# A decoder layer on one core: 24 of 26 pairs of projection blocks in seven products, the convolution by channel groups, and one weight sum per pair made by an adding DMA

## The chip, the core and the metric

The kernel runs on one core of a Trainium2 chip. TensorE (PE) multiplies matrices, with its weight loads shown apart (PEld); VectorE (DVE), ScalarE (ACT) and GpSimd (POOL) do element-wise work; SyncE (SP) issues most of the transfers, GpSimd some of them. The metric is the time on the device in microseconds (us), the median of several runs, and lower is better. Next to it stands one profiled execution with its own time; all durations of single instructions come from that one.

## What is computed

One layer: RMSNorm of x, one wide projection, three groups of heads, an output projection, a residual and a last RMSNorm. All in float32, with x of 512 tokens by 2048 features.

```python
h = rmsnorm(x, norm_g[l])
proj = h @ w_in[l]                       # 2048 -> 6664 features
(cv_a, cv_b, cv_gate, fq, fk, fv, f_logit, fox_gate,
 mq, mem_gate) = jnp.split(proj, SPLITS, axis=-1)

u = cv_a * jax.nn.sigmoid(cv_b)
u = causal_depthwise_conv(u, conv_w[l], conv_b[l])          # 31 taps, 512 channels
u = jax.nn.silu(layernorm(u, conv_ln_g[l], conv_ln_b[l]))   # over channels
y_conv = (u @ w_conv_pw[l]) * jax.nn.silu(cv_gate)

logf = jax.nn.log_sigmoid(f_logit + b_f[l])
y_fox = fox_attention(fq, fk, fv, logf) * jax.nn.silu(fox_gate)       # 8 heads, causal
y_mem = memory_attention(mq, mk, mv) * jax.nn.silu(mem_gate)          # 4 heads, 256 memory tokens
x = x + jnp.concatenate([y_conv, y_fox, y_mem], -1) @ w_out[l]
```

Before the split, `mk` and `mv` come from a projection of the normalised memory. At the end stands `rmsnorm(x, final_g)`.

## The kernel before

**Precision.** Every float32 operand is split into a high and a low part in a format that TensorE multiplies at once (`whi`/`wlo` of a weight, `hh`/`hl` of the normalised input, kept transposed as feature by token). A product is three matmuls: high by high, high by low, low by high (`mm3`, L104 to L106). A split costs a cast on ScalarE (L93) and a subtraction on VectorE (L94).

**Blocks.** The projection is 52 blocks of 128 output features, in pairs, and a narrow one for the forget logits (L407, L408). A block in the plain form (`project`) streams 512 tokens through 16 feature tiles: 16 x 3 matmuls of 512 columns. Two blocks are a pair.

**Seven products.** `pair` computes two blocks as a 2 by 2 matrix product (two halves of the 2048 features, two halves of the 512 tokens) with seven products instead of eight, each 8 feature tiles x 3 matmuls of 256 columns (`product`, L729). For it, sums of the four quarters of the input are needed in split form: `s0`, `s1`, `s2` (`first_sums`) and a fourth (`last_sum`) that is written over a quarter of the input, `hl` and `hh`, that no plain block may read after that. Each pair also makes four sums of its weights on VectorE (`less`, L699). A weight half is loaded by SyncE into one of six buffers called `raw`.

**Order.** The first 22 blocks and the forget logits run plain: convolution inputs A and B of four channel groups, memory queries, memory gates, convolution gates, and one fox pair. In that stretch the background list `bg` spreads 120 taps of the depthwise convolution (L328) and the cumulative sum of the forget logits over the projections, 6 to 8 items each; the LayerNorm over channels (`centre`, `normalise`, L489 to L514) runs beside the last memory projection, and `first_sums` and `last_sum` beside the convolution gates and the first fox pair. The other 15 pairs then run in seven products, each with the attention work of the pair before it between its products. The output projection (L978) follows.

Tiles get their buffers from pools, and a tile framework puts in the waits and orders the instructions of each engine by when it expects them to be ready. Each engine works its own list in order: an instruction that waits holds back all that stand behind it on that engine.

Of the kernel before, what the change touches and what calls it, by code (L numbers as in the profile page):

```python
# [10 lines left out]
F32 = mybir.dt.float32  # L11
# [23 lines left out]
PLAIN = 1  # L35
# [12 lines left out]
def hybrid_layer_kernel(  # L48
# [58 lines left out]

    bg = deque()
# [40 lines left out]
    cd = dr.tile([NH, S], F32, name="cd")  # L149

# [10 lines left out]
    mkv = mpool.enter_context(tc.tile_pool(name="mkv", bufs=1, side="right"))  # L161
# [5 lines left out]
    with tc.tile_pool(name="start", bufs=1) as st:  # L167
# [129 lines left out]
    def project(f0, per=0):  # L297
# [5 lines left out]
        background(per)  # L303
        return o

    def silu_of(pool, o, tag, bufs):

        sg = pool.tile([P, S], F32, tag=tag, name=nm(tag), bufs=bufs)
        nc.scalar.activation(sg, o, AF.Silu)
        return sg  # L310

# [3 lines left out]
    with tc.tile_pool(name="conv", bufs=1, reuse_waits="tile") as cp:  # L315
        cs = [tuple(cp.tile([P, S], F32R, name=f"cs{w}{c}") for w in "hl") for c in range(NC)]
        acc = [cp.tile([P, S], F32, tag=f"acc{c}", name=f"acc{c}") for c in range(NC)]

        def taps_of(c, up):
            a = acc[c]  # L320

            def first():
                nc.scalar.activation(  # L323
                    a, up[:, 0:S], AF.Identity, scale=cwt[:, c, 0:1], bias=conv_b_c(c)
                )

            def tap(j):
                return lambda: nc.vector.scalar_tensor_tensor(  # L328
                    a, up[:, j : j + S], cwt[:, c, j : j + 1], a, ALU.mult, ALU.add
                )  # L330

            bg.append(first)
            bg.extend(tap(j) for j in range(1, TAPS))

        def conv_in(c):
            oa = project(C_A + c * P, 6)
            ob = project(C_B + c * P, 6)
            up = cp.tile([P, PAD + S], F32, tag="up", name=nm("up"), bufs=3)
            nc.gpsimd.memset(up[:, 0:PAD], 0.0)
            sg = cp.tile([P, S], F32, tag="sgb", name=nm("sgb"), bufs=2)  # L340
            nc.scalar.activation(sg, ob, AF.Sigmoid)
            nc.vector.tensor_tensor(up[:, PAD:], oa, sg, ALU.mult)
            taps_of(c, up)

        def mem_query(ma, h):
            o = project(M_Q + h * P, 7)
            qh = ma.tile([P, S], F32R, tag="qh", name=nm("qh"), bufs=1)
            ql = ma.tile([P, S], F32R, tag="ql", name=nm("ql"), bufs=1)
            split(qh, ql, o)
            return qh, ql  # L350

        def mem_probs(ma, h, q):
            qh, ql = q
            pr = []
            for i2 in range(2):
                sp = at((P, 2, M))
                for j in range(2):
                    sl = slice((2 * i2 + j) * P, (2 * i2 + j + 1) * P)
                    mm3(sp[:, j, :], (qh[:, sl], ql[:, sl]), (mk[0][:, h, :], mk[1][:, h, :]), True, True)
                ng = ma.tile([P, 2], F32, tag="ng", name=nm("ng"), bufs=4)  # L360
                nc.vector.tensor_reduce(ng, sp, AX.X, ALU.max, negate=True)
                nc.vector.tensor_scalar(ng, ng, SC, None, ALU.mult)
                pp = ma.tile([P, 2, M], F32, tag="pp", name=nm("pp"), bufs=2)
                sm = ma.tile([P, 2], F32, tag="sm", name=nm("sm"), bufs=4)
                for j in range(2):
                    nc.scalar.activation(
                        pp[:, j, :], sp[:, j, :], AF.Exp,
                        bias=ng[:, j : j + 1], scale=SC, accum_out=sm[:, j : j + 1],
                    )
                nc.vector.reciprocal(sm, sm)  # L370
                for j in range(2):
                    nc.scalar.mul(pp[:, j, :], pp[:, j, :], sm[:, j : j + 1])
                pr.append(pp)
            return pr

        def mem_attend(ma, h, pr, gate):
            pts = []
            for mt in range(MT):
                tp = at()
                for i in range(NT):  # L380
                    nc.tensor.transpose(
                        tp[:, i * P : (i + 1) * P], pr[i // 2][:, i % 2, mt * P : (mt + 1) * P], ident
                    )
                th = ma.tile([P, S], F32R, tag="th", name=nm("th"), bufs=2)
                tl = ma.tile([P, S], F32R, tag="tl", name=nm("tl"), bufs=2)
                split(th, tl, tp)
                pts.append((th, tl))
            ov = at()
            for mt in range(MT):
                hs = slice(h * P, (h + 1) * P)  # L390
                mm3(ov, (mv[0][:, mt, hs], mv[1][:, mt, hs]), pts[mt], mt == 0, mt == MT - 1)
            nc.vector.tensor_tensor(gate, ov, gate, ALU.mult)
            nc.gpsimd.dma_start(out=yd[12 + h], in_=gate)

        fgs = {}

        def forget_logits(fg):
            wf = fg.tile([P, KT, NH], F32, name="wf")
# [3 lines left out]
            wfs = fg.tile([P, KT, P], F32R, name="wfs")  # L402
# [6 lines left out]
            f2 = fg.tile([2 * NH, S], F32, name="f2")  # L409
            nc.vector.tensor_copy(f2, fo[: 2 * NH, :])  # L410
            fl = fg.tile([NH, S], F32, name="fl")
            nc.gpsimd.dma_start(out=fl, in_=f2[NH : 2 * NH, :])
            fgs.update(f2=f2, fl=fl)

        def log_sigmoid(fg):
            z, e = fgs["f2"][:NH, :], fgs["fl"]
            nc.vector.tensor_tensor(z, z, e, ALU.add)
            nc.vector.tensor_scalar(z, z, bf_t, None, ALU.add)
            nc.vector.scalar_tensor_tensor(e, z, -1.0, z, ALU.mult, ALU.max)
            nc.scalar.activation(e, e, AF.Exp, scale=-1.0)  # L420
            u = fg.tile([NH, S], F32, name="u")
            nc.vector.tensor_scalar(u, e, 1.0, None, ALU.add)
            lu = fg.tile([NH, S], F32, name="lu")
            nc.scalar.activation(lu, u, AF.Ln)
            nc.vector.scalar_tensor_tensor(e, u, -1.0, e, ALU.add, ALU.subtract)
            nc.vector.reciprocal(u, u)
            nc.vector.tensor_tensor(e, e, u, ALU.mult)
            nc.vector.tensor_tensor(lu, lu, e, ALU.subtract)
            HALF = S // 2
            cs = [fg.tile([NH, HALF + S], F32, name=f"cs{i}") for i in range(2)]  # L430
            for t in cs:
                nc.vector.memset(t[:, :HALF], 0.0)
            nc.vector.scalar_tensor_tensor(cs[0][:, HALF:], z, 0.0, lu, ALU.min, ALU.subtract)
            cur, step = 0, 1

            def double(a, b, step):
                return lambda: nc.vector.tensor_tensor(
                    b[:, HALF:], a[:, HALF:], a[:, HALF - step : HALF - step + S], ALU.add
                )

            adds = []
            while step < S:
                adds.append(double(cs[cur], cs[1 - cur], step))
                cur, step = 1 - cur, 2 * step
            c = cs[cur][:, HALF:]
            adds.append(lambda: nc.gpsimd.dma_start(out=cd, in_=c))
            fgs["c"] = c
            for f in reversed(adds):
                bg.appendleft(f)

        def forget_columns():
            c = fgs["c"]
            pc = at((P, NT * NH))
            for i in range(NT):
                nc.tensor.transpose(
                    pc[:, i * NH : (i + 1) * NH], c[:, i * P : (i + 1) * P], ident[:NH, :NH]
                )
            nc.vector.tensor_scalar(ccol.rearrange("p i h -> p (i h)"), pc, -1.0, None, ALU.mult)
        conv_in(0)
        with tc.tile_pool(name="fg", bufs=1, reuse_waits="tile") as fg:  # L460
            forget_logits(fg)
            conv_in(1)
            log_sigmoid(fg)
            conv_in(2)
            forget_columns()
        conv_in(3)
        with tc.tile_pool(name="matt", bufs=1, reuse_waits="tile") as ma:

            gates = []
# [607 lines left out]
```

## Time and profile before

| | us |
|---|---|
| median of 3 runs (871.82 to 873.68) | 873.48 |
| the profiled execution: its own time | 872.15 |
| its span, first to last instruction | 870.3 |
| TensorE busy | 855.7 |
| VectorE busy | 656.8 |
| ScalarE busy | 463.8 |
| GpSimd busy | 37.9 |

Mean granted TensorE clock: 0.995. Transfers: 107.5 MB, 124 GB/s over the span. The span is 1.85 us below the time of the execution. Busy shares are means over stages with different limits, so the stretches matter more: the plain projections lie before about 350 us, the seven-product pairs from there to about 700 us, the output projection behind.

### The profile page before, as it was taken

What the parts mean: (1) busy time and instruction counts of PE and PEld (TensorE: products, weight loads), DVE (VectorE), ACT (ScalarE), POOL (GpSimd) and SP (SyncE); (2) the same over time, 40 slices, a digit from 0 to 9 for tenths busy, and PEclk for the clock granted to TensorE, in tenths of its full rate; (3) what the DMA queues carried; (4) which work ended last, traced back from release to release, by engine and by line L of the source; (5) the groups of instructions that cost most, each with busy time, mean ns of one, the idle gap of its engine ahead of it and who ended that gap; (6) DMA issues with size and microseconds to landing.
All of it is one profiled execution on the core that took longest, in us unless ns stands there. A gap on an engine that the chain in (4) does not pass through costs nothing.

```text
span 870.3 us, 13950 instructions
## 1 busy us (share of the span) xinstructions
PE 855.7 (98%) x5562; PEld 774.9 (89%) x5562; DVE 656.8 (75%) x948; ACT 463.8 (53%) x734; POOL 37.9 (4%) x76
## 2 busy tenths in 40 slices
PE   8999999999999999999999999999999999999996
PEld 6887887888888888999999999999999988998995
DVE  4656699999956987877777777777777895876964
ACT  5894342225456643577565665657574852443523
POOL 1001000000000002010001000000000000000001
PEclk9999999999999999999999999999999999999998
DMA  9972234333342334243434343333334745351415
GB/s 325 352 193 57 73 97 111 97 78 92 85 109 62 108 97 134 73 121 98 111 88 117 97 103 101 100 95 103 109 98 126 262 154 186 98 194 49 146 49 193
DMA packets 143265, 107.52 MB, mean 124 GB/s; under 512 B 3892, under 2 KB 126816, under 8 KB 142560
## 3 DMA queue, kind: packets, MB, share of 16 engines
q1 hardware_dynamic: 141696, 102.52, 40.4%
q0 software_dynamic: 1504, 4.11, 1.4%
q8 instruction: 43, 0.70, 0.3%
q14 instruction: 22, 0.18, 0.1%
HBM read 98.46 MB, written 8.14 MB: 122 GB/s over the span
## 4 chain that ended last, share of the span: by engine, by line
PE 96%; DVE 1%; issue 1%; DMA 1%; ACT 0%; SPq 0%; POOL 0%; POOLq 0%; ACTq 0%
PE pj L729 34%; PE pj L104 13%; PE pj L105 13%; PE pj L106 13%; PE pj L978 8%; PE at L104 3%; PE at L106 3%; PE at L105 3%; PE at L817 1%; DMA raw<-in_w_mem_kv_dram 1%; PE pj L262 0%; PE at L262 0%; PE pj L407 0%; PE pj L408 0%; PE at L778 0%
## 5 line engine op out<-in xcount | busy, mean ns | idle before, releaser
L93 ACT CAST whi<-raw 128x1024 fp32r<-128x1024 f32 x205 | 214.9, 1050 | 302.6 <-PE pj L105 115.1
L94 DVE TENSOR_TENSOR wlo<-raw,whi 128x1024 fp32r<-128x1024 f32 x205 | 250.2, 1222 | 121.2 <-ACT whi L93 116.7
L105 PE MATMUL pj<-hl,whi 128*128 128x512 f32 x352 | 139.6, 396 | 0.0
L106 PE MATMUL pj<-hh,wlo 128*128 128x512 f32 x352 | 139.4, 396 | 0.0
L104 PE MATMUL pj<-hh,whi 128*128 128x512 f32 x352 | 139.3, 396 | 0.0
L729 PE MATMUL pj<-hh,whi 128*128 128x256 f32 x480 | 135.4, 282 | 0.0
L729 PE MATMUL pj<-hl,whi 128*128 128x256 f32 x480 | 135.0, 281 | 0.0
L729 PE MATMUL pj<-hh,wlo 128*128 128x256 f32 x480 | 134.8, 281 | 0.0
L699 DVE TENSOR_TENSOR raw<-raw,raw 128x1024 f32<-128x1024 f32 x76 | 92.6, 1219 | 0.7
L729 PEld LDWEIGHTS pj<-hh,whi 128*128 128x128 f32 x480 | 90.5, 188 | 0.1
L729 PEld LDWEIGHTS pj<-hl,whi 128*128 128x128 f32 x480 | 90.5, 188 | 0.1
L729 PEld LDWEIGHTS pj<-hh,wlo 128*128 128x128 f32 x480 | 90.5, 188 | 0.0
L328 DVE SCALAR_TENSOR_TENSOR acc<-up,cwt,acc 128x512 f32<-128x512 f32 x120 | 84.5, 744 | 1.2 <-ACT acc L323 0.9
L978 PE MATMUL pj<-whi,rh 128*128 128x256 f32 x448 | 79.9, 279 | 0.7 <-DVE sst L1032 0.4
L104 PEld LDWEIGHTS pj<-hh,whi 128*128 128x128 f32 x352 | 66.1, 188 | 15.9 <-DVE hl L97 0.2
L106 PEld LDWEIGHTS pj<-hh,wlo 128*128 128x128 f32 x352 | 66.1, 188 | 15.7
L105 PEld LDWEIGHTS pj<-hl,whi 128*128 128x128 f32 x352 | 66.2, 188 | 15.5
L978 PEld LDWEIGHTS pj<-whi,rh 128*128 128x128 f32 x448 | 68.8, 188 | 1.3 <-DVE res L904 1.1
L978 PE MATMUL pj<-wlo,rh 128*128 128x256 f32 x224 | 62.3, 279 | 0.0
L978 PEld LDWEIGHTS pj<-wlo,rh 128*128 128x128 f32 x224 | 42.1, 188 | 0.2
L729 PE MATMUL pj<-s0l,whi 128*128 128x256 f32 x120 | 34.4, 286 | 0.0
L729 PE MATMUL pj<-s0h,whi 128*128 128x256 f32 x120 | 34.3, 286 | 0.0
(295 smaller groups left out, 1676.7 us busy)
## 6 DMA issues: line engine op xcount, KB each, us to landing
raw<-in_w_in_dram SPq DMA_DIRECT2D x104, 512.0 KB, 3.8
raw<-in_w_out_dram SPq DMA_DIRECT2D x32, 512.0 KB, 4.6
raw<-in_w_mem_kv_dram SPq DMA_DIRECT2D x12, 512.0 KB, 7.3
xr<-in_x_dram SPq DMA_DIRECT2D x4, 1024.0 KB, 7.9
res<-in_x_dram SPq DMA_DIRECT2D x8, 512.0 KB, 7.2
out_dram<-res SPq DMA_DIRECT2D x16, 256.0 KB, 2.7
rs<-yd SPq DMA_DIRECT2D x15, 256.0 KB, 4.9
mr<-in_mem_dram SPq DMA_DIRECT2D x8, 256.0 KB, 7.3
```

The source lines that it names most:

```text
L93: ins = nc.scalar.copy(hi, src)
L94: nc.vector.tensor_tensor(lo, src, hi.bitcast(F32), ALU.subtract)
L104: nc.tensor.matmul(o, ah, bh, start=start, stop=False)
L105: nc.tensor.matmul(o, ah, bl, start=False, stop=False)
L106: nc.tensor.matmul(o, al, bh, start=False, stop=stop)
L328: return lambda: nc.vector.scalar_tensor_tensor(a, up[:, j : j + S], cwt[:, c, j : j + 1], a, ALU.mult, ALU.add)
L699: nc.vector.tensor_tensor(o, p, q, ALU.subtract)
L729: nc.tensor.matmul(o, p[:, k, :], q, start=start and k == 0 and i == 0, stop=k == HK - 1 and i == 2, skip_group_check=True,)
L817: nc.tensor.transpose(tp[:, (i - j) * P : (i - j + 1) * P], pr[i][:, j * P : (j + 1) * P], ident)
L978: nc.tensor.matmul(o[:, m, :], p, q[:, k, :], start=start and k + m + i == 0, stop=k == HK - 1 and i == 2, skip_group_check=True,)
```

## The change

The plain form is left to five blocks of work: C_A0, C_B0, the forget logits, M_Q0 and M_G0. The remaining 24 pairs all run in seven products, in this order: three memory pairs, then fox pairs of queries with keys (qk) and gates with values (gv), with the pairs C_A, C_B of the other channel groups put between, then the two pairs of convolution gates (g0, g1), and the last qk and gv.

- `first_sums` for all four groups stand ahead of M_Q0 and M_G0, `last_sum` right behind them, and log-sigmoid, cumulative sum and `forget_columns` after that. All sums are thus made at the start.
- The depthwise convolution goes by channel groups: `conv_channels(c, ...)` puts 31 taps of one group on the list, of which each product of a pair takes one (`background(1)`). The accumulated group goes to DRAM (`accd`) and is loaded again (`la`) before the LayerNorm.
- `centre` and `normalise` follow g0, `project_conv` follows g1. Squares for the variance move from VectorE to ScalarE.
- A pair has five loads instead of four. One weight sum, `added`, is made by a GpSimd transfer with `accum_op=ALU.add` onto a loaded buffer, and the rest are three sums on VectorE (`plus`) along a chain.
- The scaling of the rows of x by their norm goes from ScalarE to VectorE.

```diff
-            nc.scalar.mul(xrows[t], xrows[t], rs)
+            nc.vector.tensor_scalar(xrows[t], xrows[t], rs, None, ALU.mult)
...
+    with tc.tile_pool(name="fg", bufs=1, reuse_waits="tile") as fg:
+        oa, ob = project(C_A), project(C_B)
+        conv_channels(0, [oa], ob)
+        forget_logits(fg)
+        with tc.tile_pool(name="stmp", bufs=2, reuse_waits="tile") as stmp:
...
+            for g in range(4):
+                first_sums(tmp, g)
+            oq, og = project(M_Q), project(M_G)
+            for g in range(4):
+                last_sum(tmp, g)
+        forget_columns(log_sigmoid(fg))
...
+        b11, chain, b22, b21, added = (
+            load(f, half) for f, half in ((fa, 0), (fb, 0), (fb, 1), (fa, 1), (fb, 0))
+        )
+        nc.gpsimd.dma_start(out=added, in_=rows(fb, 1), accum_op=ALU.add)
+        x1, zo, x2 = (pj((P, M)) for _ in range(3))
+        product(x1, b11, a11, start=True)
+        yield
+        nc.scalar.copy(x2, x1)
+        plus(chain, b11)
+        product(zo, chain, s1, start=True)
+        p5 = kept(zo, "p5")
+        plus(chain, b22)
+        product(x2, chain, s2)
+        u2 = kept(x2, "u2")
+        product(x1, b21, a12)
+        product(zo, b22, s4)
+        product(x2, added, s3)
+        col = pp_.tile([P, S], F32, tag="col", name=nm("col"), bufs=2)
+        negated_less(col[:, M:], x2, p5)
+        negated_less(col[:, :M], zo, u2)
+        plus(chain, b21)
+        yield
+        product(x2, chain, a22)
+        yield (x1, x2), col
...
+    def open_norm():
+        lp = ln["pool"] = lnpool.enter_context(tc.tile_pool(name="ln", bufs=1, reuse_waits="tile"))
+        background(len(bg))
+        acc = ln["acc"] = [lp.tile([P, S], F32, name=f"la{c}") for c in range(NC)]
+        for c in range(NC):
+            nc.gpsimd.dma_start(out=acc[c], in_=accd[c])
...
+            if i == 0:
+                centre()
+                normalise()
+            else:
+                project_conv()
+                lnpool.close()
+                open_fox()
...
+    work = [(M_Q + h * P, M_G + h * P, after_mem(h)) for h in range(1, NM)]
+    for h in range(NH):
+        work.append((F_Q + h * P, F_K + h * P, after_qk(h)))
+        work.append((F_G + h * P, F_V + h * P, after_gv(h)))
+        if h in (0, 2, 4):
+            c = h // 2 + 1
+            work.append((C_A + c * P, C_B + c * P, after_conv(c)))
+        if h == NH - 2:
+            for i in range(2):
+                g = C_G + 2 * i * P
+                work.append((g, g + P, after_gates(i)))
```

Three places show how the instructions move. The first is on VectorE, behind the forget matmuls. Before, the copy of the forget logits `f` is followed by taps (`acc`), the forget chain, and the splits of the next plain block's weights (`wlo`):

```order
L410 COPY f_1045<-pj_1012 16x512 [waits PE_49]
L328 SCALAR_TENSOR_TENSOR acc_872<-up_998,cwt,acc_872 128x512 [waits DVE_49] x3
L417 TENSOR_TENSOR f_1045<-f_1045,fl 8x512 [waits DMASW7_49]
L328 SCALAR_TENSOR_TENSOR acc_872<-up_998,cwt,acc_872 128x512 [waits DVE_49]
L418 TENSOR_SCALAR f_1045<-f_1045,bf_t 8x512 [waits DMASW5_49,DVE_49]
```

And now, with the temporaries `t` of `first_sums`, whose first rows read the input's parts:

```order
L396 COPY f_1025<-pj_1036 16x512 [waits PE_49]
L315 TENSOR_TENSOR t_119_1075<-hh_105,hl_106 128x512
L315 TENSOR_TENSOR t_120_1076<-hh_113,hl_114 128x512
L315 TENSOR_TENSOR t_121_1077<-hh_105,hl_106 128x512
L315 TENSOR_TENSOR t_122_1090<-hh_107,hl_108 128x512
L315 TENSOR_TENSOR t_123_1091<-hh_115,hl_116 128x512
```

All sums now stand behind the copy, and the copy waits for TensorE. Some sixty rows on, the end of the same list: the last sum's low parts (`hl`), taps, and the steps of the cumulative sum (`cs`) in turn.

```order
L93 TENSOR_TENSOR hl_110<-t_149_1271,hh_109 128x2x256
L371 SCALAR_TENSOR_TENSOR acc_1021<-up_1020,cwt,acc_1021 128x512
L93 TENSOR_TENSOR hl_112<-t_151_1278,hh_111 128x2x256
L421 TENSOR_TENSOR cs_1286<-cs_1287 8x512
L371 SCALAR_TENSOR_TENSOR acc_1021<-up_1020,cwt,acc_1021 128x512
L421 TENSOR_TENSOR cs_1287<-cs_1286 8x512
```

The second place is TensorE at the other end of these: the fifth product of the first pair in seven products, which reads `hl` as it is written, then the transposes of `cs`, then the sixth product.

```order
L500 MATMUL pj_1376<-hl_110,whi_1501 128x256 [waits DVE_49]
L500 MATMUL pj_1376<-hh_109,wlo_1502 128x256
...
L500 MATMUL pj_1376<-hl_112,whi_1501 128x256 [waits DVE_49]
L500 MATMUL pj_1376<-hh_111,wlo_1502 128x256
...
L432 MATMUL at_1311<-ident,cs_1287 128x8 [waits DVE_49]
L432 MATMUL at_1311<-ident,cs_1287 128x8 x3
L500 MATMUL pj_1377<-s2h_884,whi_1530 128x256 [waits Activation_49]
```

In TensorE's list nothing but the two plain blocks M_Q0, M_G0 and the first five products stands between the forget matmuls and these transposes. The third place is TensorE around the variance (`mean_r` multiplies by 1/512). Before, the two matmuls stand among a memory gate's projection (`pj_2383`):

```order
L483 MATMUL pj_2310<-csh_864,mean_r 128x512 [waits DVE_49]
L104 MATMUL pj_2383<-hh_101,whi_2373 128x512
L105 MATMUL pj_2383<-hl_102,whi_2373 128x512
L106 MATMUL pj_2383<-hh_101,wlo_2374 128x512
...
L484 MATMUL pj_2310<-csl_865,mean_r 128x512 [waits DVE_49]
```

Now they are followed at once by the pointwise convolution, which reads the first normalised group (`csh_7594`):

```order
L500 MATMUL pj_7248<-hh_119,wlo_7547 128x256
L615 MATMUL at_7338<-csh_7334,mean_r 128x512 [waits DVE_49]
L616 MATMUL at_7338<-csl_7335,mean_r 128x512 [waits DVE_49]
L103 MATMUL pj_7577<-csh_7594,whi_7583 128x512 [waits Activation_49]
L103 MATMUL at_7578<-csh_7594,whi_7583 128x512 [waits PE_49]
```

No product stands between the variance and that group any more.

More of the change, by code (lines that the diff above doesn't have):

```diff
@@ new lines, in hybrid_layer_kernel, with less, plus @@
+    ppool = ctx.enter_context(ExitStack())
+    pp_ = ppool.enter_context(tc.tile_pool(name="pair", bufs=1, side="right", reuse_waits="tile"))
+    a11 = [quarter(g, 0, 0) for g in range(4)]
+    a12 = [quarter(g, 1, 0) for g in range(4)]
+    a22 = [quarter(g, 1, 1) for g in range(4)]
+    s4 = [quarter(g, 0, 1) for g in range(4)]
+    s1, s2, s3 = sums
+    def less(o, p, q):
+        nc.vector.tensor_tensor(o, p, q, ALU.subtract)
+    def plus(o, p):
+        nc.vector.tensor_tensor(o, o, p, ALU.add)
```

760 lines of the change are left out of this document (356 added, 404 removed).

## The prediction

> **What bounds the kernel now.** I read the busy table first, then the chain of waits, then stretches of the program, then single engines inside those stretches.
>
> ```profile
> PE 855.7 (98%) x5562; PEld 774.9 (89%) x5562; DVE 656.8 (75%) x948; ACT 463.8 (53%) x734; POOL 37.9 (4%) x76
> PE 96%; DVE 1%; issue 1%; DMA 1%; ACT 0%; SPq 0%; POOL 0%; POOLq 0%; ACTq 0%
> ```
>
> TensorE (PE) is busy for 855.7 of 870.3 us and 96% of the chain lies on it, so the kernel is matmul time plus about 15 us of gaps. The next question is whether any other engine is close behind, and where.
>
> ```profile
> 69.00:100.00 31.00, 31.00 (x140) 24.86 (x140) 15.19 (x23) 10.62 (x14) 3.18 (x4) 1.00 0.28 70
> 100.00:150.00 50.00, 50.00 (x218) 40.10 (x217) 47.69 (x65) 16.25 (x17) 1.03 (x2) 1.00 0.33 86
> 150.00:200.00 50.00, 50.00 (x222) 40.54 (x221) 47.47 (x68) 14.54 (x16) 0.12 (x1) 1.00 0.34 89
> 250.00:300.00 50.00, 50.00 (x230) 40.84 (x229) 34.97 (x52) 30.42 (x48) 1.08 (x2) 1.00 0.33 87
> 300.00:350.00 50.00, 50.00 (x217) 40.50 (x216) 41.44 (x60) 19.84 (x30) 5.44 (x8) 1.00 0.38 109
> 400.00:450.00 50.00, 50.00 (x414) 49.65 (x413) 37.98 (x58) 33.11 (x59) 2.17 (x5) 1.00 0.36 96
> ```
>
> Columns: length, then busy time of PE, weight load, VectorE (DVE), ScalarE, GpSimd, then PE clock, DMA share, GB/s. PE is full in every one of them. DVE is not far off: 47.7 and 47.5 of 50 us while the convolution taps run (100 to 200), and 41.4 while the input sums are made (300 to 350). The kernel before has room for its DVE work only because it is spread over hundreds of microseconds of plain projections. The change removes most plain projections, so DVE is what I follow.
>
> **The matmul saving.**
>
> ```profile
> 73.48 0.47 PE pj L104 x2
> 430.65 14.20 PE pj L729 x120
> ```
>
> On the chain, two 512-column matmuls take 0.47 us, 0.2335 each to more places, and 120 of 256 columns take 14.20, 0.1183 each. A plain pair is 96 of the first, 22.4 us; a pair in seven products is 7 x 8 x 3 = 168 of the second, 19.9 us. Nine more pairs take the second form (24 instead of 15): 864 x 0.2335 = 201.7 us go, 1512 x 0.1183 = 178.9 come, a saving of 22.9 us. Every other matmul is as before. If nothing else waited, that would be all.
>
> **The sums at the start.** Before, the four groups of sums of the normalised input were needed at about 340 us. Now the first pair that needs them comes right after five plain blocks' work (C_A0, C_B0, forget logits, M_Q, M_G). In VectorE's new order all sums, the log-sigmoid chain and the taps of channel group 0 stand behind the copy of the forget logits, which waits for the forget matmuls. Call their end t_F.
>
> ```profile
> 100.17 0.39 PE L408 MATMUL pj<-hl,wfs 128*128 128x512 f32 x1
> 100.40 0.40 PE L104 MATMUL pj<-hh,whi 128*128 128x512 f32 x1
> ```
>
> t_F was 100.4 before and should be near that again, since the same blocks stand ahead. From t_F to the first consumer that needs them all (the transposes of forget columns ahead of the sixth product), VectorE has 52 element-wise operations of 128x512 of the sums, 11 of 128x1024 (8 splits of weights, 3 weight sums), 18 taps, and 19 operations of the forget chain, one of them a reciprocal. Prices by their starts in the queue:
>
> ```profile
> 107.10 1.23 DVE L94 TENSOR_TENSOR wlo<-raw,whi 128x1024 fp32r<-128x1024 f32 x1
> 108.24 0.75 DVE L328 SCALAR_TENSOR_TENSOR acc<-up,cwt,acc 128x512 f32<-128x512 f32 x1
> ...
> 109.38 0.73 DVE L328 SCALAR_TENSOR_TENSOR acc<-up,cwt,acc 128x512 f32<-128x512 f32 x1
> 110.04 0.67 DVE L425 SCALAR_TENSOR_TENSOR fl<-u,fl 8x512 f32<-8x512 f32 x1
> 110.65 0.73 DVE L328 SCALAR_TENSOR_TENSOR acc<-up,cwt,acc 128x512 f32<-128x512 f32 x1
> 111.31 3.33 DVE L426 RECIPROCAL u<-u 8x512 f32<-8x512 f32 x1
> 114.57 0.64 DVE L328 SCALAR_TENSOR_TENSOR acc<-up,cwt,acc 128x512 f32<-128x512 f32 x1
> ```
> ```profile
> 303.60 0.68 DVE L556 TENSOR_TENSOR t<-hh,hl 128x512 f32<-128x512 f32 x1
> 304.20 0.69 DVE L94 TENSOR_TENSOR s1l<-t,s1h 128x512 fp32r<-128x512 f32 x1
> 304.93 0.69 DVE L556 TENSOR_TENSOR t<-hh,hl 128x512 f32<-128x512 f32 x1
> 305.65 0.69 DVE L562 TENSOR_TENSOR t<-t,t 128x512 f32<-128x512 f32 x1
> ```
>
> From start to start: a wide one 1.14, a tap 0.66, a small one 0.61, the reciprocal 3.26, an element-wise one of the sums 0.60 or, mostly behind a dependent one, 0.72; I take 0.66. The sums are 52 x 0.66 = 34.3, the wide ones 11 x 1.14 = 12.5, the taps 18 x 0.66 = 11.9, the forget chain 3.3 and 18 small ones, some shorter than 0.61, 10.2: together 72 us. With 0.60 it is 69, with every full duration 78. In the same time PE has M_Q and M_G (22.4), and of the first pair five products of 24 x 0.1183 = 2.84: 36.6 us. So PE, which ran out of nothing here before, waits 72 - 36.6 = **35 us** (32 to 41). The least I can think of: if half of the taps and forget operations were not ahead of the last sums, 13 us fewer, so 22. The stall does not come back: PE stays the bound afterwards and VectorE's early finish buys nothing.
>
> **The LayerNorm over channels.** Before, its chain ran beside memory projections with PE full (250 to 300 above). Now the gate pair g0 is followed by centring and normalising, and g1 by the pointwise convolution, whose first matmul stands directly behind the variance matmuls in PE's order: PE has nothing between.
>
> ```profile
> L505 ACT ACT_TABLE_LOAD x1 | 1.3, 1283 | 0.0
> L506 ACT ACTIVATE up<-up 128x512 f32<-128x512 f32 x1 | 0.6, 635 | 0.0
> L514 ACT ACTIVATE acc<-acc,cols 128x512 f32<-128x512 f32 x4 | 3.2, 824 | 0.0
> L93 ACT CAST csh<-acc 128x512 fp32r<-128x512 f32 x4 | 2.3, 617 | 0.0
> L507 DVE TENSOR_TENSOR up<-up,up 128x512 f32<-128x512 f32 x1 | 0.7, 693 | 0.7 <-ACT up L506 0.7
> L511 DVE TENSOR_TENSOR acc<-acc,up 128x512 f32<-128x512 f32 x4 | 2.5, 686 | 0.0
> ```
>
> Add epsilon 0.4; Ln and Exp, each a table load and 0.63, 3.8; three operations on VectorE 2.1; the product with the first group 0.7; a table load and Silu 2.1; the cast 0.6: 9.7 us, plus about 0.8 of handing over, **10.5 us** (6 if table loads run ahead in the waits, 14 if VectorE is behind).
>
> **The adding DMA.** One weight sum of each pair leaves VectorE; in its place come a fifth load and a GpSimd transfer that adds 512 KB onto it.
>
> ```profile
> raw<-in_w_in_dram SPq DMA_DIRECT2D x104, 512.0 KB, 3.8
> rv<-in_w_mem_kv_dram SPq DMA_DIRECT2D x4, 512.0 KB, 8.1
> wf<-in_w_in_dram POOLq DMA_DIRECT2D x1, 64.0 KB, 3.8
> L699 DVE TENSOR_TENSOR raw<-raw,raw 128x1024 f32<-128x1024 f32 x76 | 92.6, 1219 | 0.7
> ```
>
> The trace has no adding transfer. Bounds: 3.8 us, as a plain load; 8.1, as 512 KB on a crowded queue. The sum is needed by the pair's sixth product, and its buffer comes free with the sixth product of the pair before, some 20 us earlier (a pair's PE time); cast and split (2.3), load (3.8) and issue take up about 7, so about 13 are left. I take nothing; beyond 13, each microsecond is paid in 23 pairs. In the steady pairs VectorE has 3 instead of 4 sums of 1.22, plus 7 taps (4.6): 38.0 of 50 us before becomes 15 to 21 us per pair of 20 to 24 us of PE. It fits, narrowly in three pairs with nine taps, so nothing either (0 to 4 in all). The Trainium skill, page "Collectives: The Full Stack", says of its reduction that the add needs two source reads where a copy needs one; by an estimate from that, twice the 3.8 us, 7.6, would fit as well; no run here shows an adding transfer.
>
> **Small ones.** The row scaling of x moves from ScalarE to VectorE, where PE idled at 62 to 66 us:
>
> ```profile
> 62.00:64.00 2.00, 0.56 (x6) 0.32 (x3) 1.75 (x4) 2.00 (x4) 0.00 (x0) 1.00 0.97 247
> 64.00:66.00 2.00, 1.59 (x11) 1.12 (x11) 2.00 (x5) 2.00 (x4) 0.00 (x0) 1.00 1.00 262
> ```
>
> At most 1.9 us; I take -1. Against it, the clock:
>
> ```profile
> 6.00:8.00 2.00, 0.53 (x5) 0.29 (x3) 0.00 (x0) 0.44 (x1) 0.00 (x0) 1.00 1.03 373
> 8.00:10.00 2.00, 0.96 (x2) 0.58 (x3) 1.36 (x2) 2.00 (x5) 0.00 (x0) 0.63 1.06 400
> 10.00:12.00 2.00, 2.00 (x7) 1.61 (x7) 2.00 (x4) 1.04 (x3) 0.00 (x0) 0.51 1.05 409
> 12.00:14.00 2.00, 2.00 (x10) 1.57 (x10) 1.55 (x3) 1.02 (x2) 0.00 (x0) 1.00 1.05 385
> ```
>
> After PE stood still around 7 us, the granted clock was 0.63 and 0.51 for 4 us: 2 x 0.37 + 2 x 0.49 = 1.7 us of work lost. Two long waits at least, the start and the LayerNorm, make +3 (0 to 6). The same rows show 385 to 409 GB/s; a new pair asks for 6 x 512 KB in 20 us, some 160, so loads have room. The Trainium skill, "TensorE: Matmul & The Clock Gate", Part 1, states a rule that speaks against this change: after an idle window of about 3.4 us PE drops to half clock, and needs about as long busy to return. By that rule each long wait costs an estimated 1.7 us more; the rows at 8 to 12 us agree.
>
> **Sum.** The profiled execution took 872.15 us. 872.15 - 22.9 + 35 + 10.5 - 1 + 3 = 896.8. The median of the runs, 873.48, is 1.3 above the profiled one, the smallest of my errors; I forecast **896 us**, rounded down, with an own range of 880 to 914 from the bounds of the terms.
>
> **Rivals.**
>
> (1) *Faster.* PE waits at neither place and only the saving counts: 872.15 - 22.9 = 849.3, with some waits 850 to 858. For it: PE is 96% of the chain, and the same sums were hidden before. Against: they were hidden under 250 us of plain work, and 69 us of queue do not fit into 37. It decides if the sums' work ahead of the last sum is under about 40 us. Chance 0.14.
>
> (2) *The start costs half.* Splits and sums run ahead of taps and the forget chain, or the LayerNorm finds PE work: 22 + 5 in place of 45.5 give 878, and 868 if each is a little less. Chance 0.13.
>
> (3) *The adding DMA is slow.* With several transfers beside it, it takes 15 to 17 us; sixth products wait 2 to 4 us in 23 pairs, 46 to 92 more: 920 to 985. For it: GpSimd's queue is in order and holds mask operations and stores of outputs ahead of some of these transfers, so one late store delays an add. Against: the DMA share in the steady pairs was 0.36. Slower, chance 0.10.
>
> (4) *The change does not do what it says*, the extra pairs being bound by VectorE (94% of the PE time in three pairs): the 22.9 us are not gained, 872 + 47.5 = 920. Chance 0.05.
>
> The forecast has 0.58.
>
> **How the numbers follow.** Changes under 0.2% (1.7 us) cannot be told from none here. Faster: all of (1) and a quarter of (2), 0.17; same: 0.04; slower: 0.79. The range that leaves 2 in 10 out takes half of (2), the own range and the beginning of (3): 864 to 918.
>
> **What would show it.** Right: PE busy near 833 us and idle of 50 us or more; in the stretch from 100 to 175 us VectorE full and PE half idle, its waits named by the sums' low parts (s0l, s1l, hl) and the cumulative sum; a PE gap of about 10 us right before the pointwise convolution, granted clock under 1 after both; from 200 to 700 us PE full. Wrong: PE full at 100 to 175 us (rival 1); the first weight split of each sixth product ended by a DMA on GpSimd's queue (rival 3); gaps at the chain sums in every pair (rival 4).

## The result, and the profile after

The changed kernel takes 925.51 us (four runs, 921.98 to 927.12) against 873.3 for the kernel before beside it: 1.060 times as long, 95% interval 1.056 to 1.063. It is slower, as forecast, but by 52 us and not by 23: the forecast of 896 and its range of 864 to 918 are both missed.

The first three fences are of the kernel after. The busy table and the beginning of the chain by engine:

```profile
PE 849.9 (92%) x6210; PEld 802.8 (87%) x6210; DVE 705.9 (76%) x1013; ACT 511.2 (55%) x805; POOL 88.3 (10%) x108
PE 62%; DVE 13%; DMA 10%; ACT 7%; issue 7%; POOL 0%; SPq 0%; ACTq 0%; POOLq 0%; DVEq 0%
```

TensorE's share of the chain fell from 96% to 62%. Its idle time in the span of 924.0 us is 74.1 us, where it was 14.6 of 870.3. Busy time fell by 5.8 us and not by 22.9, since matmuls at half clock and the first ones after each wait last longer. Transfers, which had 1% of the chain, have 10%; the forecast had nothing for them.

The windows in which TensorE is not full, with columns as in the prediction:

```profile
125.00:150.00 25.00, 11.48 (x60) 10.07 (x60) 25.00 (x34) 8.83 (x11) 0.00 (x0) 0.70 0.25 63
150.00:175.00 25.00, 11.33 (x74) 11.09 (x75) 24.86 (x40) 7.49 (x11) 2.11 (x2) 0.61 0.33 55
...
650.00:675.00 25.00, 19.45 (x143) 18.86 (x142) 19.73 (x25) 10.86 (x16) 1.60 (x1) 0.86 0.48 111
675.00:700.00 25.00, 10.28 (x50) 8.58 (x49) 12.78 (x17) 12.24 (x16) 0.00 (x0) 0.73 0.26 63
```

At the start VectorE is full, TensorE has less than half of its time and the clock is 0.70 and 0.61. At 650 to 700 us, around the LayerNorm, TensorE is idle for 20.3 us: 14.7 of it are its own two waits (`csh`, `csl` below), and 5.4 belong to a weight split of the pair ahead of it. And what TensorE waited for, in total, times, and longest:

```profile
PE pj L500 <- ACT p L471: 14.7, 1, 14.7
PE pj L103 <- ACT csh L92: 10.1, 1, 10.1
PE pj L500 <- DVE wlo L93: 9.5, 9, 2.0
...
PE pj L500 <- DVE s1l L93: 4.9, 1, 4.9
PE at L616 <- DVE csl L613: 4.6, 1, 4.6
```

The first is the fifth product at the start (the copy that it is put down to stands in ScalarE's list behind the casts of the last sum), the second the pointwise convolution, the third belongs to the steady pairs.

### The profile page after: what moved, and what is told of

Its sections match the earlier page's. It is cut to its first block, busy times and chain, and to the rows that moved or that the text cites. A ratio compares the mean times of both kernels' runs of the same rounds, so it can differ in the third digit from the quotient of the medians.

```text
span 924.0 us, 15570 instructions
## 1 busy us (share of the span) xinstructions
PE 849.9 (92%) x6210; PEld 802.8 (87%) x6210; DVE 705.9 (76%) x1013; ACT 511.2 (55%) x805; POOL 88.3 (10%) x108
## 3 DMA queue, kind: packets, MB, share of 16 engines
q0 software_dynamic: 27104, 18.79, 13.4%
## 4 chain that ended last, share of the span: by engine, by line
PE 62%; DVE 13%; DMA 10%; ACT 7%; issue 7%; POOL 0%; SPq 0%; ACTq 0%; POOLq 0%; DVEq 0%
PE pj L500 31%; PE pj L1013 7%; DMA raw<-in_w_in_dram 7%; PE pj L103 4%; PE pj L104 4%; PE pj L105 4%; DVE wlo L93 4%; PE at L103 3%; PE at L105 3%; PE at L104 3%; ACT whi L92 2%; DVE acc L371 2%; DMA yd<-mgate 1%; DVE raw L467 1%; ACT L803 1%
## 5 line engine op out<-in xcount | busy, mean ns | idle before, releaser
L500 PE MATMUL pj<-hh,whi 128*128 128x256 f32 x768 | 218.5, 285 | 15.5 <-ACT p L471 14.7
L500 PE MATMUL pj<-hh,wlo 128*128 128x256 f32 x768 | 217.3, 283 | 0.0
L500 PE MATMUL pj<-hl,whi 128*128 128x256 f32 x768 | 217.1, 283 | 0.0
L509 POOL DMA_DIRECT2D raw<-in_w_in_dram x24 | 37.7, 1570 | 359.6 <-DMA raw<-in_w_in_dram 104.3
L500 PE MATMUL pj<-s1h,wlo 128*128 128x256 f32 x192 | 58.1, 303 | 9.5 <-DVE wlo L93 9.5
L500 PE MATMUL pj<-s1h,whi 128*128 128x256 f32 x192 | 56.8, 296 | 9.5 <-ACT whi L92 7.3
L500 PE MATMUL pj<-s1l,whi 128*128 128x256 f32 x192 | 56.6, 295 | 4.9 <-DVE s1l L93 4.9
L500 PE MATMUL pj<-s0h,wlo 128*128 128x256 f32 x192 | 54.3, 283 | 0.0
L500 PE MATMUL pj<-s2h,whi 128*128 128x256 f32 x192 | 54.1, 282 | 0.0
L500 PE MATMUL pj<-s2h,wlo 128*128 128x256 f32 x192 | 54.1, 282 | 0.0
```

The source lines that it names most:

```text
L500: nc.tensor.matmul(o, p[:, k, :], q, start=start and k == 0 and i == 0, stop=k == HK - 1 and i == 2, skip_group_check=True,)
L509: nc.gpsimd.dma_start(out=added, in_=rows(fb, 1), accum_op=ALU.add)
```

## The experiments

Three suspects: VectorE's queue at the start, the LayerNorm's chain, and the steady pairs with their adding transfers, which the prediction had priced at nothing. First, one run each, and two for the start.

**Taps left out.**

```diff
-        bg.extend(tap(j) for j in range(1, TAPS))
+        bg.extend(tap(j) for j in range(1, TAPS if c else 1))
```

> The 30 taps of channel group 0 are left out (its convolution is not computed), so VectorE's list between the forget logits and the last sum loses 17 taps of 0.66 us. Theory A (VectorE's queue at the start sets the stall): that stretch goes from 65 us to about 54, the wait ahead of the fifth product shrinks by 11 us, and the kernel takes 912 to 915. Theory B (the wait there is on something else, a transfer, the reciprocal or ScalarE's list): no change, 924 to 926.

Measured: 922.64 us. The fifth product starts at 156.1 us and not at 163.7, and its wait falls from 14.7 to 10.3, so the place is right. The gain of 2.9 us lies within the spread of the change's four runs and in neither theory's range: of the 7.5 us, little or nothing reaches the end. In the trace the first memory head's softmax now makes TensorE wait (1.6), and the steady pairs have 5 us more of idle time between 300 and 650 us than after has (15.2 against 10.0), with the same instructions. So what is gained at the start is in part spent further on; what is near the bound there comes below.

**More cover.**

```diff
-            oq, og = project(M_Q), project(M_G)
-            for g in range(4):
-                last_sum(tmp, g)
...
+    for h in range(3):
+        oq, og = project(M_Q + h * P), project(M_G + h * P)
+        after_mem(h)([oq], og)
+    for g in range(4):
+        last_sum(tmp, g)
...
-    work = [(M_Q + h * P, M_G + h * P, after_mem(h)) for h in range(1, NM)]
+    work = [(M_Q + h * P, M_G + h * P, after_mem(h)) for h in range(3, NM)]
```

> Two more memory pairs run plain (22 pairs in seven products instead of 24), and the last sum comes after them, so TensorE has 45 us more of work that needs no sums. Matmuls cost 2 x 2.54 = 5.1 us more. Theory A (VectorE's queue): the queue to the last sum grows from 67 to about 106 us because it takes in the splits of the added blocks, TensorE's cover from 36 to about 85, so the stall falls from 32 to about 20 and the half clock goes: 925 - 12 - 3 + 5 = 915. Theory B (the wait is on something that does not move with cover): 930.

Measured: 917.54. Eight microseconds better with 5.1 more of matmuls; the stall moves with the cover, as theory A has it. TensorE's longest wait at the start is now 8.5 us for the cumulative sum. Two pairs fewer also mean two adding transfers fewer, about 2 us by the price found below.

**Pointwise convolution one pair later.**

```diff
     def after_qk(h):
-        return lambda xs, col: pr.update({h: probs(h, *queries_keys(xs, col))})
+        def f(xs, col):
+            if h == NH - 1:
+                project_conv()
+                lnpool.close()
+                open_fox()
+            pr.update({h: probs(h, *queries_keys(xs, col))})
+        return f
```

and the same three calls go from the work that follows g1.

> The pointwise convolution moves one pair later, to the beginning of the work that follows qk7, so that a pair's 20 us of products stands between the variance matmuls and it. Theory A (TensorE stands still there only because nothing is left to do): the 14.7 us of idle time between 675 and 700 us and about 3 us of half clock go, 907 to 910. Theory B (the load of the pointwise weights or the loads of the convolution groups are late whatever stands there): at most 5 us come back, 920.

Measured: 917.40. The wait for `csh` falls from 10.1 to 1.5 us and that for `csl` is gone, so the 14.7 us were the missing work behind the variance. Eight of them reach the end, less than theory A's 15 to 18 and more than theory B's 5. Its waits of TensorE show what stayed and grew:

```profile
PE pj L500 <- DVE wlo L93: 11.8, 12, 3.0
PE pj L500 <- ACT whi L92: 7.6, 4, 5.4
```

The 5.4 us is the third product of the pair g1: its weight sum waits for a load that takes 10.8 us in the kernel after, while an adding transfer, a store and four reloads of convolution groups are on the way. That belongs to the next suspect.

**The sum on VectorE in place of the adding transfer.**

```diff
-        nc.gpsimd.dma_start(out=added, in_=rows(fb, 1), accum_op=ALU.add)
...
         plus(chain, b22)
+        plus(added, b22)
```

> The adding transfer becomes a sum on VectorE, as a fourth sum per pair; the fifth load stays. Theory A (the adding transfers delay the plain loads beside them and cost most of the 13 us of waits between 175 and 650 us, and 5 at 650): 910 to 916, though VectorE has 29 us more work. Theory B (VectorE is close to the bound in these pairs, and the transfer does what it is meant to): waits for VectorE grow, 925 to 945.

Measured: 912.07 (909.45 to 914.69), 13 us better although VectorE is busy 23.5 us longer. The edit that was to relieve VectorE costs more than the work that it takes away.

**Neither of the two.** The same without the added line.

> The adding transfer is left out with nothing in its place, so one of the seven products of each pair uses an incomplete weight sum. VectorE keeps three sums per pair, the fifth load stays. If the adding transfer costs time by itself and a fourth sum on VectorE is free: the same as with the sum on VectorE, 908 to 914, idle time of TensorE between 175 and 650 us near 5. If the fourth sum costs too: 898 to 906. If the adding transfer costs nothing and the gain with the sum on VectorE came from elsewhere: 920 to 926.

Measured: 899.04. So the adding transfer costs 26.5 us, where the prediction had nothing, and a fourth sum on VectorE 13.0 (10 to 16 by the spread of the two runs with it). In the steady pairs (280 to 630 us), first the kernel after, then this one:

```profile
280.00:630.00 350.00, 339.30 (x2782) 334.96 (x2782) 289.31 (x409) 224.79 (x350) 46.01 (x50) 1.00 0.66 147
```
```profile
280.00:630.00 350.00, 350.00 (x2910) 348.17 (x2909) 298.02 (x418) 219.87 (x348) 25.69 (x38) 1.00 0.50 136
```

Without the transfer TensorE is never idle and does 128 matmuls more in the same time; the share of the transfer engines falls from 0.66 to 0.50. Which product waits is in the groups of after by form, 300 to 600 us:

```profile
L500 PE MATMUL pj<-s1h,wlo 128*128 128x256 f32 x104 | 31.0, 298 | 7.9 <-DVE wlo L93 7.9
...
L500 PE MATMUL pj<-s2h,whi 128*128 128x256 f32 x104 | 29.2, 281 | 0.0
```

`s2` is the sixth product, the one that uses the added sum: it never waits. `s1` is the third, which uses the second sum along the chain, made by VectorE from plain loads. VectorE's waits for those loads, between 275 and 640 us, in after and in the run without the transfer:

```profile
DVE raw L467 <- DMA raw<-in_w_in_dram: 21.1, 10, 4.5
```
```profile
DVE raw L467 <- DMA raw<-in_w_in_dram: 6.5, 5, 2.1
```

The adding transfer is in time for its own product: no cast and no split waits for it anywhere. It makes other loads late. In the kernel after, 15 sums wait for a load between 175 and 660 us; 14 of these loads are on the way together with an adding transfer and take 5.4 to 10.8 us, while the 46 loads from 280 to 630 us without one beside them take 3.9 (median). Most loads are hardly slower, 4.3 us against 4.2 in the run without the transfer (medians of that stretch); it is the few that a sum waits for that count. VectorE's list is in order, so a sum that waits for a load holds the splits behind it.

**All that only moves the sums.** Two runs tried to take the stall at the start by order alone. In the first, the first sums are written ahead of C_A0; in the second the forget logits also come behind M_G0, and the taps of group 0 last. The lines of the first (its temporaries get a pool at each of the two places):

```diff
+            for g in range(4):
+                first_sums(tmp, g)
         oa, ob = project(C_A), project(C_B)
...
         forget_logits(fg)
...
-            for g in range(4):
-                first_sums(tmp, g)
             oq, og = project(M_Q), project(M_G)
```

> The sums that need no plain block's result (the first three of each group) are written ahead of C_A0 instead of behind the forget logits, so VectorE's list can take them from about 70 us on, beside C_A0, C_B0 and the forget matmuls; matmuls are the same. Behind the copy of the forget logits stand 35 operations, about 25 us, in place of 97. Theory A (the queue behind the copy is the stall): PE's wait at the start falls from 28 us idle and 5 of half clock to under 8: 897 to 903. Theory B (the work is only moved and VectorE is late all the same): 915 to 925.

Measured: 915.46, ten us better than the change and in theory B's range.

> The first sums ahead of C_A0 as in the run with early sums, and the forget logits behind M_G0 in place of ahead of M_Q0, so that the split of their weights no longer holds TensorE while the sums are made; taps of group 0 are written last. Theory A (VectorE's queue, which in the run with early sums only moved its wait of 21 us to the forget matmuls): the wait there goes, some 10 us stay at the fifth product, 900 to 906. Theory B: the wait turns up again at another place, 912 to 918.

Measured: 926.78, no better than the change and outside both ranges. TensorE's waits at the start, first of the one with early sums, then of the other:

```profile
PE pj L395 <- DVE wfs L94: 21.0, 1, 21.0
```
```profile
PE pj L505 <- ACT p L476: 8.6, 1, 8.6
PE pj L394 <- DVE wfs L93: 5.8, 1, 5.8
PE pj L505 <- DVE col L109: 2.7, 1, 2.7
```

`wfs` is the split of the forget weights, now behind the sums in VectorE's list; the room for these weights is also taken over from the temporaries of the sums, which is my edit's doing: with early sums their load is issued at 104.0 us and not at 61.3. So the run is no clean test of the order alone. The wait turns up where the first result of VectorE is needed. In the kernel after, VectorE is busy for 95 us between 60 us and the transposes at 169, and TensorE's matmuls there are worth 74 at full clock (37.5 to t_F, 36.6 behind it). Early sums fill VectorE's free time between 60 and 100 us (busy 38.1 of 40 us, 26.6 before the edit), which goes with the ten us gained; the difference of some 21 us stays as long as all of this work stands ahead of the transposes. Why the second order loses the ten us again was not traced.

**Combinations.** Sum on VectorE with the later convolution, and the two with early sums.

> Sum on VectorE and pointwise convolution one pair later. If the two losses are apart, the gains add: 925 - 13 - 8 = 904. If both are the same crowd of transfers at 640 to 680 us: 909 to 912.

Measured: 907.18, between the two; the later convolution brings 4.9 here, not 8, so the two losses may overlap in part (the two runs with the sum on VectorE are 5 us apart, so this is rough).

> The two and the early sums. If the three losses are apart and the early sums take the stall away: 904 - 25 = 879, near the kernel before; all that is then left of the 22.9 us of matmul time would be eaten by shorter waits. If the losses overlap: 890 to 900.

Measured: 901.64, 5.5 for the early sums and short of both forecasts: the early sums take little of the stall away, as above.

**What is dear in the transfer.** It stays, but writes and does not add:

```diff
-        nc.gpsimd.dma_start(out=added, in_=rows(fb, 1), accum_op=ALU.add)
+        nc.gpsimd.dma_start(out=added, in_=rows(fb, 1))
```

> The GpSimd transfer stays, from the same queue and on the same buffer behind the same load, but it writes and does not add, so one weight sum lacks a part. Theory A (it is the adding that is dear: by the queue's share of the transfer engines an adding 512 KB occupies them for 4.4 us, a plain one 1.8): most of the 26 us go, 902 to 908, landing near 4 us. Theory B (the chain of load, GpSimd's queue and landing holds a buffer too long, whatever the transfer does): little changes, 919 to 926.

Measured: 907.13. Of the 26.5 us the addition as such has 18.4, as theory A has it; another 8.1 is the price of a plain transfer of 512 KB more per pair. Issues and queue of GpSimd's transfers, adding first (packets, MB, share of 16 engines; the last row of each has KB and us to landing):

```profile
q0 software_dynamic: 27104, 18.79, 13.4%
...
raw<-in_w_in_dram POOLq DMA_DIRECT2D x24, 512.0 KB, 7.9
```
```profile
q0 software_dynamic: 5600, 18.79, 6.6%
...
raw<-in_w_in_dram POOLq DMA_DIRECT2D x24, 512.0 KB, 5.0
```

Without the transfer the queue has 2144 packets and 1.9%. So 24 adding transfers make 24,960 packets, 1040 each, and take 13.4% of 924.0 less 1.9% of 896.2, which is 107 us of all 16 engines, 4.4 each. A plain one makes 144 packets and takes 6.6% of 905.7 less the same, 1.8 each. Adding the same bytes occupies the engines 2.5 times as long. The landing (5.0 for 7.9 us) and GpSimd's time for the issue fall with it, so this run does not show how much of the 18.4 us each of the three has.

**The sum on GpSimd itself.**

```diff
-        nc.gpsimd.dma_start(out=added, in_=rows(fb, 1), accum_op=ALU.add)
+        nc.gpsimd.tensor_tensor(added, added, b22, ALU.add)
```

> The sum is made on GpSimd itself as an element-wise operation, neither by a transfer nor on VectorE. If GpSimd does 128x1024 in under some 6 us and disturbs nobody: as without the sum, 899 to 903. If it is slow or slows VectorE: 905 to 925.

Measured: 917.66, worse than on VectorE. One operation takes 2.6 us, and TensorE waits 5.0 us for column results between 275 and 640 us, where it waits for nothing without the sum. What GpSimd holds up is VectorE. The same splits, first with the sum on GpSimd, then without it:

```profile
L93 DVE TENSOR_TENSOR wlo<-raw,whi 128x1024 fp32r<-128x1024 f32 x232 | 309.0, 1335 | 87.3 <-ACT whi L92 86.7
```
```profile
L93 DVE TENSOR_TENSOR wlo<-raw,whi 128x1024 fp32r<-128x1024 f32 x232 | 282.5, 1222 | 97.4 <-ACT whi L92 96.7
```

VectorE runs the same 1013 instructions and is busy for 737.0 us in place of 705.7. Of the 25 splits that ran while GpSimd added, 18 took 1.6 to 3.4 us, where 1.22 is the rule. So 24 sums on GpSimd cost VectorE 31 us, more than the 29 us of doing them itself.

> The order of the run before, the pointwise convolution one pair later, and the sum on GpSimd. If the three losses add up and GpSimd's sum is free: 925 - 22 - 8 - 25 = 870, level with the kernel before. If GpSimd's sum costs what VectorE's does: 883.

("The run before" is the second of the two orders, with the forget logits behind M_G0.) Measured: 906.12, far above both forecasts, which rested on gains that do not exist: by their own runs the order brings nothing, and the sum on GpSimd 7.9 us and not 25.

**Is the saving there at all?** The sums of the input left out (the products take quarters of the input), first alone, then with no adding transfer and the later convolution:

```diff
-            for g in range(4):
-                first_sums(tmp, g)
             oq, og = project(M_Q), project(M_G)
-            for g in range(4):
-                last_sum(tmp, g)
...
-    s1, s2, s3 = sums
+    s1, s2, s3 = a11, a22, a12
```

> The 52 operations of the input sums are left out (the products take quarters of the input in their place, so the projections are not what they should be); taps, forget chain, adding transfers and the order of pairs stay. Theory A (VectorE's amount of work in the start sets the stall): VectorE's list behind the forget logits falls from 72 to about 37 us, TensorE's cover is 36.6, so the stall of 35 us goes but for 0 to 4: 887 to 892. Theory B (something else at the start, the forget chain, a transfer, the first use of the split sums): 905 to 925.

Measured: 903.29, a gain of 22.2, just below theory B's range and far from A's; yet what A names is what happened. The stall at the fifth product is gone: TensorE is idle for 5.0 us between 97.5 and 175 us, and the largest waits left are 3.3 us for the cumulative sum and 1.7 behind the gate activation of the first memory head. Part of the gain is lost in the steady pairs, as without the taps: 14.2 us idle between 300 and 650 us against 10.0.

> All three suspected causes are taken away: the sums of the input, the adding transfer with nothing in its place, and the pointwise convolution one pair later. Matmuls are all there. If the saving of 22.9 us in matmuls is real and the three are the whole loss: 850 to 857 (849.3 by the sum, and some short waits). If the nine added pairs gain less than their count of matmuls says, or a fourth loss exists: 863 or more.

Measured: 860.85, 0.986 of the kernel before (0.983 to 0.989): 12 us faster than it, 65 faster than the change. Its busy table, and its longest waits of TensorE:

```profile
PE 837.6 (98%) x6210; PEld 794.2 (92%) x6210; DVE 674.5 (79%) x961; ACT 495.2 (58%) x784; POOL 50.0 (6%) x84
```
```profile
PE pj L103 <- ACT mh L95: 3.0, 1, 3.0
PE pj L496 <- ACT whi L92: 1.5, 1, 1.5
PE at L432 <- DVE cs L421: 1.5, 1, 1.5
PE pj L496 <- ACT pj L508: 1.5, 1, 1.5
```

TensorE's busy time is 18.1 us under that of before, and its share is 98% again. It does the matmuls of the changed kernel, so most of the saving is there. The time lies between the two forecasts, 11.5 above the 849.3 of the sum: TensorE is idle for 21.3 us, 6.7 more than before, in many short waits of which the longest is 3.0, and its matmuls take 4.8 us more than 855.7 - 22.9, at a mean clock of 0.991 (0.995 before). No single fourth loss of any size is left.

The three losses are not independent. Taken away one at a time they bring 22.2, 8.1 and 26.5, together 56.8; taken away at once 64.7. Once the adding transfers are gone, the start and the LayerNorm bring 38.2 together (899.04 to 860.85), where beside the transfers they bring 30.3 one by one. TensorE is idle for 1.8 us between 300 and 650 us here, and for 14.2 in the run without the input sums: the steady pairs eat a part of a gain at the start only beside the adding transfers.

None of the versions that compute the layer in full beats the kernel before: the best is 901.64.

## Why the prediction was wrong, step by step

**What bounds the kernel before: right.** A full TensorE with VectorE close behind it was the reading from which the slowdown follows, and after the change TensorE waits for VectorE.

**The matmul saving, 22.9 us: there in the main.** With the causes taken away the same matmuls end 12 us under the kernel before; the other 11 us go to short waits (6.7) and to matmuls that take longer than counted (4.8).

**The start, 35 us: right in size and place.** The forecast was 72 us from the end of the forget matmuls to the transposes of the forget columns. The first and last rows in the kernel after (min, median and max in ns, then first and last start):

```profile
L395 PE MATMUL pj<-hl,wfs x16: 395/395/395, 90.3 to 97.3; 128*128 128x512 f32 x16
```
```profile
L432 PE MATMUL at<-ident,cs x4: 202/218/271, 169.1 to 169.4; 8*128 8x8 f32 x4
```

Since a matmul takes 0.2335, t_F is 97.5: 71.6 us, and less the cover of 36.6, 35.0. VectorE ran 103 instructions there, where 100 were counted, and was busy for 71.0 of the 71.6 us, so the mechanism is right too. Of the 35.0, 27.8 are idle time of TensorE and 7.2 are matmuls that took longer (busy 43.8 us in place of 36.6), most of it by the clock. What the forecast did not know: a stall of 35 us taken away is not worth 35 us. Leaving the sums out gave 22.2, because the stall also covered other lateness, the cumulative sum (3.3) and the first memory head's gate (1.7) among it, and because the steady pairs behind it, with their adding transfers, ate another part.

**The LayerNorm, 10.5 us: right for the chain, short by the load.** The wait for `csh` is 10.1. That it agrees to 0.4 is partly luck: the table load for Silu (1.28) ran ahead of the chain, and the first cast stood behind the second group's activation in ScalarE's list. Ahead of the chain stand 4.6 for `csl`: its subtraction is queued on VectorE behind the split of the pointwise weights, whose load lands late. In the end the whole was worth 8.1.

**The clock, 3 us: right in kind, too small.** The start alone has the 7.2 us above, which the reading of 35.0 contains. In the windows above it is granted at 0.70, 0.61, 0.86 and 0.73. The 24 matmuls of the fifth product, 2.84 us at full clock, took 5.49. The Trainium skill, "TensorE: Matmul & The Clock Gate", Part 1, has the same: idle for a window, then half clock. The trace agrees: after waits, 0.50 from 144 to 164 us.

**The scaling of x, -1: right in kind.** TensorE's idle time at 62 to 66 us went from 1.85 to 0.03, and t_F came 2.9 us earlier (97.5 for 100.4).

**The adding DMA, "I take nothing": the step that failed.** It measured 26.5 us. The duration was bounded well, 3.8 to 8.1, with 7.9 measured in the median (6.6 to 9.1). The slack of 13 us was also right: the sixth product never waits. What was wrong is what I asked, whether the transfer is in time for its own user. It is, and it occupies the engines for 4.4 us of each pair's 20, so that the loads beside it, on which the chain of sums hangs, come late (how much of this is time on the engines and how much the longer landing was not separated): VectorE's sums wait 21.1 us for loads between 275 and 640 us, and 6.5 without it. So the sign named for the forecast, TensorE full from 200 to 700 us, failed as well. Rival 3 had the right culprit and the wrong place (sixth products). That 925.5 lies in its range of 920 to 985 says little, since its own 46 to 92 us would give 942 to 988. Rival 4's sign, gaps at the chain sums, was seen in part, and its 920 is near, but its cause is not: without the transfers TensorE does not wait for VectorE there. The evidence against rival 3, a share of 0.36, was read as a mean of room, where a load that is needed at a certain time is what counts. The Trainium skill, "Collectives: The Full Stack", Part 3, says that the add in its reduction needs two source reads. The estimate of 7.6 that was made from it is close to the 7.9 partly by luck: the plain write from the same queue landed after 5.0, and twice that is 10.

**VectorE in the steady pairs, "0 to 4 in all": right, and narrow.** Without the adding transfer VectorE makes three sums per pair, and TensorE waits for nothing between 175 and 640 us. A fourth sum of 1.22 us per pair, 29 us of work, already costs 13 us. The room that was left, 15 to 21 of 20 to 24 us, is therefore no cover to count on.

Put together: 872.2 - 22.9 + 35.0 + 14.7 - 2.9 + 26.5 = 922.6, and 925.7 was the time of the profiled execution; the clock at the start is inside the 35.0. At the LayerNorm 8.3 us of matmuls ran at half clock (654.0 to 660.8 and 681.3 to 695.0), an estimated 4 us lost, about what the sum is short of. The terms are not quite apart (the run without the transfer also has 5 to 7 us less idle time at the LayerNorm), so the sum closes better than it has a right to: taken away one at a time, the start gave 22.2 and the LayerNorm 8.1.

Without the adding transfer the kernel takes 899, within 3 us of the forecast, and that is partly luck. By the runs, the start and the LayerNorm are then worth 38.2 us, where the forecast had 48.5 with the clock; and the nine added pairs with the row scaling bring 12.3 us (873.1 to 860.85), where it had 23.9. The two differences, 10 and 12 us, nearly cancel.

## What to carry to other kernels

When work is moved from an engine to a transfer, ask not only whether the transfer is in time for its own result, but what other transfers, needed sooner, it makes late; here adding took the engines 2.5 times as long as writing the same bytes, and three times the microseconds (26.5 against 8.1). When a stage is removed, list what had been hidden under it: here 250 us of plain projections hid some 70 us of VectorE's queue, and neither of two other orders of the same work in the shorter stretch hid it again. The length of a stall is not yet what its removal brings: 35 us gave 22, and more only once the next loss was gone too.

## What the runs showed of the hardware that I had not expected

An adding transfer of 512 KB was cut into 1040 packets where the plain one had 144, took 4.4 us of all 16 engines where the plain one took 1.8, landed after 7.9 us (median) where the plain one took 5.0, and kept GpSimd 1.57 us for its issue where the plain one took 0.90:

```profile
L509 POOL DMA_DIRECT2D raw<-in_w_in_dram x24 | 37.7, 1570 | 359.6 <-DMA raw<-in_w_in_dram 104.3 <-DVE col L109 88.2 <-DVE t L109 52.8
```
```profile
L509 POOL DMA_DIRECT2D raw<-in_w_in_dram x24 | 21.5, 897 | 351.9 <-DVE col L109 88.4 <-DVE wlo L93 57.3 <-DVE cs L421 50.6
```

Other transfers of GpSimd's queue suffered with it: stores of 256 KB (`yd<-fgate`) that landed after 2.4 us in the kernel before took 7.1; with the plain write it was 4.9, and with no transfer there 3.4. An element-wise sum of 128x1024 on GpSimd takes 2.6 us, on VectorE 1.2, and while it runs a split on VectorE took up to 3.4 us in place of 1.2.
